# A two-half S5 scan on VectorE: steps in two parts, another order of the work around them, and one weight load issued by ScalarE

## The chip, the cores and the metric

The kernel runs on one core of a Trainium2 chip. A core has five engines that take instructions from queues of their own and wait for each other by semaphores: TensorE (PE) for matrix products, VectorE (DVE), ScalarE (ACT), GpSimd (POOL) and SyncE (SP, which here only issues transfers). The metric is the time of one execution on the device, in microseconds; less is better.

## The reference

A decoder trunk of two layers on 256 tokens of 2048 channels, in float32. Layer 0 is an S5 mixer (a diagonal complex recurrence), layer 1 attention in a sliding window; each is followed by a gated feed-forward network, with root-mean-square norms ahead of every block. The diff touches the S5 mixer alone:

```python
def s5_mixer(u, a_re, a_im, log_step, b_re, b_im, c_re, c_im, d_skip, w_glu):
    ...                                    # lb = exp(a * dt), bb = (lb - 1) / a * b: complex, 128 groups x 64 states
    bu_re = jnp.einsum('blgc,gpc->blgp', uc, bb_re)
    bu_im = jnp.einsum('blgc,gpc->blgp', uc, bb_im)
    ...                                    # s[l] = lb * s[l-1] + bu[l] along the 256 tokens
    y = jnp.einsum('blgp,gcp->blgc', s_re, cr_) - jnp.einsum('blgp,gcp->blgc', s_im, ci_)
    y = y + d_skip.astype(f32) * uf
    g = jax.nn.gelu(y).astype(u.dtype)
    gl = g @ w_glu
    out = gl[..., :dm] * jax.nn.sigmoid(gl[..., dm:])
```

## The kernel before

**Large products.** Every weight is read as pieces of 512 x 512 (`raw`, two buffers, 1 MB each), split into an upper part (`W.high`, ScalarE, line 122) and a lower part (`W.low`, VectorE or GpSimd, line 127), and multiplied with the split activations in three products (lines 922, 923 and 924), 24 matmuls of 128x512 for a piece. `W.load` issues the load of a piece on the sync queue, line 109. From the end of the S5 mixer to the end of the kernel TensorE runs these products.

**S5.** The recurrence is taken in blocks of L = 4 tokens, so there are 64 block states and 62 steps that do work. What enters each block is made on TensorE: `turned_x` transposes the tables X (tile `px`), `tokens` the normed input (tile `pu`), `added` makes the products (tile `pv`), and `kept` copies them into the tiles V0 and V1, one half of the groups each, 4 x 4 copies. The norm's scale r0 comes from sums of squares (`rb`), and `scaled` applies it together with the norm's weights, spread over the partitions by two matmuls into the tile `gb`.

**The scan.** `step(hf)` does one step of half `hf` on VectorE: a multiply of the last state with four tables (line 573; 128 x 128 into the half's PSUM tile `scan`), and two adds into the next state (lines 576 and 578; 128 x 64 each). V0 can start earlier than V1; LEAD = 20 says how far it may be ahead in the code. `copies` moves finished states to the tiles `St` (ScalarE).

**What follows the scan.** For quarters q of the groups: `own_tokens(q)` adds what the block's own tokens give (tile `py`, line 776), `outputs(q)` what the states give (line 798), `activated` is the gelu, `turned` transposes the result (tile `pt`, line 813) and splits it into `gt` (casts on ScalarE, line 820; lower halves on VectorE, line 821). Quarters 0 and 2 belong to V0, 1 and 3 to V1. `early_piece` begins the first linear with the quarters that are there.

**Order.** Tile's dependency tracking sets the semaphores; a scheduler orders what is not pinned. Inside S5 the wrapper `Ordered` (line 210) pins instructions to the order in which the code has them while `on` is true.

Of the kernel before, what the change touches and what calls it, by code (L numbers as in the profile page):

```python
# [9 lines left out]
F32 = mybir.dt.float32  # L10
# [3 lines left out]
ALU = mybir.AluOpType  # L14
# [3 lines left out]
P = 128  # L18
# [11 lines left out]
GC = 16  # L30
# [26 lines left out]
def kernel(  # L57
# [22 lines left out]
    def bank(shape, name="ps"):  # L80
        return ps.tile(shape, F32, tag="ps", name=nm(name))
# [9 lines left out]
    class Weights:  # L91
        def __init__(self):
# [4 lines left out]
            self.limit = 0  # L97

        def add(self, ap):
            self.src.append(ap)  # L100

        def load(self, upto):
            while len(self.raw) < min(upto, len(self.src)):
                i = len(self.raw)
                if i in self.early:
                    t = self.early[i]()
                else:
                    t = pp.tile([P, 4, 512], F32, tag="raw", name=nm("raw"), bufs=2)
                nc.sync.dma_start(t, self.src[i].rearrange("(a p) n -> p a n", p=P))
                self.raw.append(t)  # L110
# [83 lines left out]
    def s5(early_piece):  # L194
# [3 lines left out]
        with st:  # L198
# [24 lines left out]

            Vt = [sp.tile([P, NK, 2, 32], F32, tag=f"V{hf}", name=f"V{hf}") for hf in range(2)]

# [66 lines left out]
            S.copy(Bn[:, 2], Bn[:, 0])  # L292


            gb = [bank([P, 512], "gb") for _ in range(2)]
            for hf in range(2):
                PE.matmul(gb[hf], sel.rearrange("p k h -> p (k h)"), nrow[:, 512 * hf : 512 * hf + 512],
                          start=True, stop=True)

# [81 lines left out]
            V.tensor_scalar(nr, LP[:, 0, 0], -1.0, None, ALU.add)  # L381
            PL.tensor_tensor(u, LP[:, 0, 1], aim, op=ALU.mult)
            PL.tensor_tensor(t, nr, are, op=ALU.mult)
            PL.tensor_tensor(w, nr, aim, op=ALU.mult)
            PL.tensor_tensor(t, t, u, op=ALU.add)
            PL.tensor_tensor(u, LP[:, 0, 1], are, op=ALU.mult)
            PL.tensor_tensor(q_[:, 0], t, iv, op=ALU.mult)
            PL.tensor_tensor(u, u, w, op=ALU.subtract)
            PL.tensor_tensor(q_[:, 1], u, iv, op=ALU.mult)


# [26 lines left out]
            squares(2)  # L418
            turned_b(B2, 1, negated)
            for i in (2, 3):  # L420
                turned_b(B2, i, lambda o, v: V.tensor_scalar(o, v, sgn[:, 1:2], None, ALU.mult))
# [58 lines left out]
            PE.matmul(pss, both.rearrange("p a k -> p (a k)"), ssq, start=True, stop=True)  # L480

            r0, rv2, ry2 = (sp.tile([P, L], F32, name=f"r{i}") for i in range(3))
            token(0, 2)
# [38 lines left out]
            tokens(0, 1)  # L522
            last_token(1)

# [21 lines left out]
            def kept(t, b, copy):  # L546
                p0 = 16 * (b // 2) + 8 * (t % 2) + 4 * (b % 2)
                copy(Vt[t // 2][:, 1:, :, p0 : p0 + 4], pvs[t, b].rearrange("p r a k -> p k r a")[:, : NK - 1])

# [4 lines left out]
            def scan_tables(hf):  # L554
                scan.append(bank([P, 2, 2, 2, 32], "scan"))
                re, im = (LPT[:, 3, ri].rearrange("p (h f a) -> p f h a", h=2, f=2)[:, hf] for ri in range(2))
                for o, v, f in ((0, re, 1.0), (1, re, 1.0), (2, im, 1.0), (3, im, -1.0)):
                    S.mul(scan[hf][:, 0, o // 2, o % 2].rearrange("p (h a) -> p h a", h=2), v, f)

# [36 lines left out]
            turned_x(0, 0)  # L596
            turned_x(0, 1)
            imag_and_tokens(1)
            added(0, 0)
# [38 lines left out]
            PL.tensor_tensor(Cq[:, :, 1], Cq[:, :, 1], c2[:, :, 0], op=ALU.add)  # L638

            lead(4)  # L640
            last_token(2)
# [4 lines left out]
            added(2, 0)  # L646
            kept(2, 0, S.copy)
            turned_x(2, 2)
            added(2, 1)
# [22 lines left out]
            kept(3, 2, S.copy)  # L672

            pc = bank([P, PAIRS], "pc")
            PE.transpose(pc, drows.rearrange("a g j c -> a (g j c)"), ident[:PAIRS, :PAIRS])
            dcol = lp.tile([P, PAIRS], F32, name="dcol")
            S.copy(dcol, pc)
            dd = lp.tile([P, PAIRS, GC], F32, name="dd")
            PL.tensor_tensor(dd, bc(dcol, 2, GC), bc(idm, 1, PAIRS), op=ALU.mult)
# [103 lines left out]
            def copied(q, k0, k1):  # L783
                a = q // 2 * 16
                return S.copy(St[q][:, :, :, k0:k1], Vt[q % 2][:, k0:k1, :, a : a + 16].rearrange("p k r a -> p r a k"))

# [39 lines left out]

            def end(a, b, between=lambda: None):
# [25 lines left out]
            while reached[0] < NK - 1:  # L853
                step(0)
                if reached[0] + 1 in cuts:
# [442 lines left out]
```

## Time and profile before

| | us |
|---|---|
| time, median of 3 runs | 2014.27 (2013.39 to 2014.71) |
| time of the profiled execution | 2014.75 |
| its span, first to last instruction | 2013.0 |
| TensorE busy | 1971.2 (98%) |
| VectorE busy | 1087.0 (54%) |
| ScalarE busy | 857.9 (43%) |
| GpSimd busy | 103.4 (5%) |

The shares are means over the whole span. They mix the first 140 us, in which the S5 mixer is worked out, with 1870 us of products.

### The profile page before, as it was taken

Reading aid. Unit: us, or ns where it says so; the run is one execution under the profiler, and the core shown is the slowest. Engines: PE = TensorE matmul, PEld = TensorE weight load, DVE = VectorE, ACT = ScalarE, POOL = GpSimd, SP = SyncE. Lnnn points to the kernel's source line nnn. Section 1 sums busy time; section 2 is a strip of 40 time slices with the busy share of each in tenths; the row PEclk is TensorE's granted clock in tenths of the full one; section 3 lists DMA queues with packets and bytes.
Section 4 is the critical chain, followed back from the end, with each engine's and each line's share of the span. In section 5 each row is a group of like instructions: output and inputs, shape, how many; then the busy total and the mean of one; then the engine's idle time right before and its main releaser. Section 6 shows DMA issues by size and latency. Waiting matters only on the chain.

```text
span 2013.0 us, 25105 instructions
## 1 busy us (share of the span) xinstructions
PE 1971.2 (98%) x10640; PEld 1633.5 (81%) x10640; DVE 1087.0 (54%) x1343; ACT 857.9 (43%) x871; POOL 103.4 (5%) x77
## 2 busy tenths in 40 slices
PE   7699999999999999999999999999999999999998
PEld 6577888888888888888888888888888888888886
DVE  8964555444444454454566885544454445444445
ACT  6554444333334333433455554433333343343333
POOL 6850000000000000000000000000000000000000
PEclk9899999999999999999999999999999999999999
DMA  4037665565566565555554435566556555655564
GB/s 129 23 109 230 202 202 190 188 188 188 188 189 190 190 198 192 190 188 188 181 196 159 151 126 169 188 189 190 192 192 198 188 188 189 190 190 192 192 198 146
DMA packets 183316, 360.62 MB, mean 179 GB/s; under 512 B 10402, under 2 KB 10466, under 8 KB 183076
## 3 DMA queue, kind: packets, MB, share of 16 engines
q1 hardware_dynamic: 182192, 355.56, 54.8%
q8 instruction: 83, 1.36, 0.3%
q10 hardware_dynamic: 580, 2.14, 0.3%
q0 software_dynamic: 432, 1.33, 0.2%
q14 instruction: 29, 0.24, 0.0%
HBM read 356.90 MB, written 2.10 MB: 178 GB/s over the span
## 4 chain that ended last, share of the span: by engine, by line
PE 93%; DVE 5%; DMA 1%; ACT 1%; issue 0%; POOL 0%; DVEq 0%; ACTq 0%
PE acc L922 29%; PE acc L924 29%; PE acc L923 29%; DVE scan L573 1%; PE tr L1061 1%; DVE V L578 1%; DVE V L576 1%; DMA raw<-in_s_w_glu_dram 1%; DVE w L127 1%; PE pv L210 1%; PE tr L966 1%; PE tr L1196 1%; PE py L798 0%; PE at L1166 0%; PE px L210 0%
## 5 line engine op out<-in xcount | busy, mean ns | idle before, releaser
L127 DVE TENSOR_TENSOR w<-raw,w 128x2048 fp32r<-128x2048 f32 x330 | 757.1, 2294 | 826.3 <-ACT w L122 826.2
L122 ACT ACTIVATE w<-raw 128x2048 fp32r<-128x2048 f32 x332 | 636.2, 1916 | 983.2 <-PE acc L924 834.1
L922 PE MATMUL acc<-w,xT 128*128 128x512 f32 x1568 | 613.1, 391 | 0.0
L924 PE MATMUL acc<-w,xT 128*128 128x512 f32 x1568 | 610.5, 389 | 0.0
L923 PE MATMUL acc<-w,xT 128*128 128x512 f32 x1568 | 610.2, 389 | 0.0
L922 PEld LDWEIGHTS acc<-w,xT 128*128 128x128 f32 x1568 | 294.4, 188 | 62.6 <-issue 2.3
L924 PEld LDWEIGHTS acc<-w,xT 128*128 128x128 f32 x1568 | 294.3, 188 | 61.5
L923 PEld LDWEIGHTS acc<-w,xT 128*128 128x128 f32 x1568 | 294.5, 188 | 60.3
L922 PE MATMUL acc<-w,hT 128*128 128x512 f32 x704 | 275.2, 391 | 0.0
L923 PE MATMUL acc<-w,hT 128*128 128x512 f32 x704 | 273.6, 389 | 0.0
L924 PE MATMUL acc<-w,hT 128*128 128x512 f32 x704 | 273.4, 389 | 0.0
L922 PEld LDWEIGHTS acc<-w,hT 128*128 128x128 f32 x704 | 132.2, 188 | 28.1 <-ACT hT L1063 1.2
L924 PEld LDWEIGHTS acc<-w,hT 128*128 128x128 f32 x704 | 132.1, 188 | 27.6
L923 PEld LDWEIGHTS acc<-w,hT 128*128 128x128 f32 x704 | 132.2, 188 | 27.0
L923 PE MATMUL acc<-w,gt 128*128 128x512 f32 x256 | 99.8, 390 | 0.6 <-DVE w L127 0.6
L922 PE MATMUL acc<-w,gt 128*128 128x512 f32 x256 | 100.1, 392 | 0.0
L924 PE MATMUL acc<-w,gt 128*128 128x512 f32 x256 | 99.7, 389 | 0.0
L923 PEld LDWEIGHTS acc<-w,gt 128*128 128x128 f32 x256 | 48.1, 188 | 10.8 <-DVE w L127 1.0
L1088 DVE TENSOR_TENSOR h<-h,acc 128x512 f32<-128x512 f32 x64 | 43.5, 687 | 24.4 <-PE acc L924 24.4
L924 PEld LDWEIGHTS acc<-w,gt 128*128 128x128 f32 x256 | 48.1, 188 | 10.0
L922 PEld LDWEIGHTS acc<-w,gt 128*128 128x128 f32 x256 | 48.1, 188 | 9.9
L1074 ACT ACTIVATE act<-acc,ry 128x512 f32<-128x512 f32 x44 | 30.1, 690 | 59.9 <-PE acc L924 59.9
(242 smaller groups left out, 1204.6 us busy)
## 6 DMA issues: line engine op xcount, KB each, us to landing
raw<-in_ffn_w_gate_dram SPq DMA_DIRECT2D x88, 1024.0 KB, 5.2
raw<-in_ffn_w_up_dram SPq DMA_DIRECT2D x88, 1024.0 KB, 5.2
raw<-in_ffn_w_down_dram SPq DMA_DIRECT2D x88, 1024.0 KB, 5.1
raw<-in_s_w_glu_dram SPq DMA_DIRECT2D x32, 1024.0 KB, 5.3
raw<-in_attn_w_qkv_dram SPq DMA_DIRECT2D x20, 1024.0 KB, 5.1
raw<-in_attn_w_o_dram SPq DMA_DIRECT2D x16, 1024.0 KB, 5.0
xk<-in_x_dram SPq DMA_DIRECT2D x4, 512.0 KB, 7.1
h<-in_x_dram SPq DMA_DIRECT2D x8, 256.0 KB, 5.8
```

Of the source, the lines that this page charges most:

```text
L122: keep(S.activation(w[:, 0], self.raw[i], AF.Copy))
L127: keep(e.tensor_tensor(lo, self.raw[i], hi.bitcast(F32), op=ALU.subtract))
L210: return (lambda *a, **k: pin(f(*a, **k))) if self.on else f
L573: keep(V.tensor_tensor(t_, ws[..., part], bc(Vt[hf][:, k - 1, :, part], 1, 2), op=ALU.mult))
L576: V.tensor_tensor(v, v, t_[:, 0], op=ALU.add)
L578: V.tensor_tensor(v, v, t_[:, 1, ::-1], op=ALU.add)
L922: keep(PE.matmul(acc, x_[:, 0], w[0][:, a], start=first, stop=False))
L923: PE.matmul(acc, x_[:, 0], w[1][:, a], start=False, stop=False)
L924: PE.matmul(acc, x_[:, 1], w[0][:, a], start=False, stop=last)
L966: PE.transpose(pt[:, t], h[t][:, kt * P : (kt + 1) * P], ident)
L1074: S.activation(s, pg[t], AF.Silu, scale=r[0][:, t : t + 1])
L1088: V.tensor_tensor(hc, hc, acc[t], op=ALU.add)
```

## The change

Four things. First, the tiles V0, V1 and `scan` get an axis of two parts of 16 columns that lie apart, and `step(hf, 2)` does a step in two parts: two multiplies of 128 x 64 and four adds of 128 x 32. V0's steps ahead of V1's first and V1's steps after V0's last are done so; where both run, steps stay whole. Second, things move: the two matmuls on the norm's weights (`gb`) behind the one for the sums of squares, one eviction of B2 from ScalarE to VectorE, the q chain on GpSimd, `last_token(1)`, the small transpose `pc` with `dcol` and `dd`, and the splitting of weight piece 0 into the middle of V1's inputs; the last X tokens are pinned ahead of the first step. Third, the load of weight piece 5 is held back (`hold`) and issued by ScalarE inside `end(1, 3)`. Fourth, with all this the scheduler puts TensorE's work at the end of the scan in another order.

```diff
@@ Weights
+            self.hold = 5
-        def load(self, upto):
-            while len(self.raw) < min(upto, len(self.src)):
+        def load(self, upto, e=nc.sync):
+            while len(self.raw) < min(upto, len(self.src), self.hold):
...
-                nc.sync.dma_start(t, self.src[i].rearrange("(a p) n -> p a n", p=P))
+                ins = e.dma_start(t, self.src[i].rearrange("(a p) n -> p a n", p=P))
+                if e is not nc.sync:
+                    tc.keep_in_program_order(ins)
@@ s5
-            Vt = [sp.tile([P, NK, 2, 32], F32, tag=f"V{hf}", name=f"V{hf}") for hf in range(2)]
+            Vt = [sp.tile([P, NK, 2, 2, 16], F32, tag=f"V{hf}", name=f"V{hf}") for hf in range(2)]
...
-            turned_b(B2, 1, negated)
-            for i in (2, 3):
+            for i in (1, 2, 3):
                 turned_b(B2, i, lambda o, v: V.tensor_scalar(o, v, sgn[:, 1:2], None, ALU.mult))
...
             PE.matmul(pss, both.rearrange("p a k -> p (a k)"), ssq, start=True, stop=True)
+            gb = [bank([P, 512], "gb") for _ in range(2)]
+            for hf in range(2):
+                PE.matmul(gb[hf], sel.rearrange("p k h -> p (k h)"), nrow[:, 512 * hf : 512 * hf + 512],
+                          start=True, stop=True)
...
-                scan.append(bank([P, 2, 2, 2, 32], "scan"))
+                scan.append(bank([P, 2, 2, 2, 2, 16], "scan"))
...
-                n = 32 // parts
-                ws, pr = scan[hf][:, 0], scan[hf][:, 1]
-                vs = []
-                for i in range(parts):
-                    part = slice(n * i, n * (i + 1))
-                    t_ = pr[..., part]
-                    keep(V.tensor_tensor(t_, ws[..., part], bc(Vt[hf][:, k - 1, :, part], 1, 2), op=ALU.mult))
-                    vs.append((Vt[hf][:, k, :, part], t_))
-                for v, t_ in vs:
-                    V.tensor_tensor(v, v, t_[:, 0], op=ALU.add)
-                for v, t_ in vs:
-                    V.tensor_tensor(v, v, t_[:, 1, ::-1], op=ALU.add)
+                each = [slice(i, i + 1) for i in range(2)] if parts == 2 else [slice(0, 2)]
+                for p in each:
+                    ws, pr = (scan[hf][:, i, p].rearrange("p h l r a -> p h l (r a)") for i in range(2))
+                    last = Vt[hf][:, k - 1, p].rearrange("p h r a -> p h (r a)")
+                    keep(V.tensor_tensor(pr, ws, bc(last, 2, 2), op=ALU.mult))
+                for l in range(2):
+                    for p in each:
+                        v, pr = Vt[hf][:, k, p], scan[hf][:, 1, p, l]
+                        V.tensor_tensor(v, v, pr[:, :, ::-1] if l else pr, op=ALU.add)

             def lead(n):
                 for i in range(n):
-                    step(0)
+                    step(0, 2, pin if i == 0 else lambda ins: ins)
...
+            imag_and_tokens(3)
             V.on = False
-            imag_and_tokens(3)
...
+            pc = bank([P, PAIRS], "pc")
+            PE.transpose(pc, drows.rearrange("a g j c -> a (g j c)"), ident[:PAIRS, :PAIRS])
+            dcol = lp.tile([P, PAIRS], F32, name="dcol")
+            S.copy(dcol, pc)
...
             kept(2, 0, S.copy)
+            W.high(0, pin)
+            W.low(0, pin, PL)
...
             kept(3, 3, S.copy)
             lead(2)
-            W.high(0, pin)
-            W.low(0, pin, PL)
...
                 outputs(b, (0,))
                 split_outputs(a, ya)
+                then()
                 outputs(b, (1,), pin)
...
             while reached[0] < NK - 1:
-                step(0)
+                step(0, 1 if reached[1] > 1 else 2)
...
-                    step(1, keep=pin)
+                    step(1, 2, pin)
...
+            def load():
+
+                W.hold = len(W.src)
+                W.load(6, nc.scalar)
+
-            last = end(1, 3, lambda: own_tokens(3))
+            last = end(1, 3, lambda: own_tokens(3), load)
```

The order of the built programs, at three places. In these rows V_77 is V0, V_78 is V1, the tile `scan` with the lower number belongs to V0, "waits DVE_49" is a wait for VectorE's own count, and "x2" two rows that read alike.

VectorE, a step of V1 after V0's last. Before:

```order
L573 TENSOR_TENSOR scan_805<-scan_805,V_78 128x128 [waits DVE_49]
L576 TENSOR_TENSOR V_78<-V_78,scan_805 128x64 [waits DVE_49]
L578 TENSOR_TENSOR V_78<-V_78,scan_805 128x64 [waits DVE_49]
```

With the change:

```order
L564 TENSOR_TENSOR scan_837<-scan_837,V_78 128x64 [waits DVE_49] x2
L568 TENSOR_TENSOR V_78<-V_78,scan_837 128x32 [waits DVE_49]
L568 TENSOR_TENSOR V_78<-V_78,scan_837 128x32
L568 TENSOR_TENSOR V_78<-V_78,scan_837 128x32 [waits DVE_49] x2
```

Six instructions stand for three, and five of them wait for VectorE's count. The second multiply waits for the count that the first one raises, the first add for that of the second multiply.

VectorE, where V1's first multiply comes in (it waits for ScalarE's copy). Before, behind V0's sixteenth step:

```order
L573 TENSOR_TENSOR scan_593<-scan_593,V_77 128x128 [waits DVE_49]
L573 TENSOR_TENSOR scan_805<-scan_805,V_78 128x128 [waits Activation_49]
L576 TENSOR_TENSOR V_77<-V_77,scan_593 128x64 [waits DVE_49]
L576 TENSOR_TENSOR V_78<-V_78,scan_805 128x64 [waits DVE_49]
L578 TENSOR_TENSOR V_77<-V_77,scan_593 128x64 [waits DVE_49]
```

With the change, behind V0's twelfth step:

```order
L564 TENSOR_TENSOR scan_593<-scan_593,V_77 128x64 [waits DVE_49] x2
L564 TENSOR_TENSOR scan_837<-scan_837,V_78 128x128 [waits Activation_49]
L568 TENSOR_TENSOR V_77<-V_77,scan_593 128x32 [waits DVE_49]
L568 TENSOR_TENSOR V_77<-V_77,scan_593 128x32
L568 TENSOR_TENSOR V_77<-V_77,scan_593 128x32 [waits DVE_49] x2
L568 TENSOR_TENSOR V_78<-V_78,scan_837 128x64
```

V1 comes in three steps of V0 earlier in the order, and the first nine steps of V1 stand beside steps of V0 in two parts; then follow 32 pairs of whole steps and nine whole steps of V0 alone.

TensorE, from own_tokens(3) and outputs(1) on (py_2048/2049 and py_2170/2171 are the tiles of quarter 3, T_1223 and T_1268 the tables of quarter 1; lines of what repeats are left out). Before:

```order
L798 MATMUL py_1942<-T_1223,St_1842 64x64 [waits Activation_49,Pool_49]
...
L776 MATMUL py_2048<-M_1443,U 64x64 [waits PE_49]
...
L798 MATMUL py_2048<-T_1232,St_1843 64x64 [waits Activation_49,Pool_49]
...
L813 MATMUL pt_2114<-ident,y_2042 128x128 [waits PE_49,Activation_49]
...
L922 MATMUL acc_1914<-w_1839,gt_1816 128x512
L923 MATMUL acc_1914<-w_1839,gt_1816 128x512 [waits Pool_49]
...
L813 MATMUL pt_2181<-ident,y_2161 128x128 [waits DVE_49,Activation_49]
```

With the change:

```order
L775 MATMUL py_2170<-M_1506,U 64x64 [waits PE_49]
...
L927 MATMUL acc_2038<-w_1929,gt_1906 128x512 [waits Activation_49]
L928 MATMUL acc_2038<-w_1929,gt_1906 128x512 [waits Pool_49]
...
L775 MATMUL py_2171<-M_1506,U 64x64 [waits DVE_49]
L796 MATMUL py_2064<-T_1268,St_1932 64x64 [waits Activation_49]
...
L811 MATMUL pt_2236<-ident,y_2164 128x128 [waits PE_49,Activation_49]
...
L927 MATMUL acc_1883<-w_174_2098,gt_2241 128x512 [waits Activation_49]
...
L811 MATMUL pt_2307<-ident,y_2285 128x128 [waits DVE_49,Activation_49]
```

Sixteen matmuls of own_tokens(3), 12 products of weight piece 3 (w_1839 before, w_1929 now) and three more of own_tokens(3), the first of which waits for VectorE, now stand ahead of outputs(1); the other 12 products of that piece stand behind the last transposes.

## Rows read from the trace of the kernel before

**Rows 1.** Busy time by stage, us from the span's start. Columns: length, then busy us and (in brackets) instructions of PE, PEld (weight loads), DVE, ACT and POOL, the granted clock of TensorE, DMA share, GB/s.

```profile
39.40:56.50 17.10, 15.44 (x321) 13.28 (x321) 12.65 (x50) 12.83 (x29) 5.57 (x3) 1.00 0.21 64
56.50:94.30 37.80, 22.56 (x420) 19.65 (x416) 37.70 (x245) 18.44 (x26) 36.60 (x18) 0.82 0.09 30
200.00:1000.00 800.00, 800.00 (x3585) 663.16 (x3584) 389.84 (x244) 315.09 (x222) 0.00 (x0) 1.00 0.60 192
```

**Rows 2.** The chain that ended last, followed back from 141 us, its shares of that stretch by engine and line.

```profile
by line: DVE scan L573 18.2%; DVE V L578 12.5%; DVE V L576 12.3%; PE pv L210 8.9%; PE py L798 5.7%; issue 5.3%; DVE w L127 5.2%; PE px L210 4.2%; DVE gt L821 2.6%; PE pu L210 2.1%; DMA ls<-in_s_log_step_dram 1.5%; PE pt L813 1.5%; ACT scan 
```

**Rows 3.** VectorE's instructions in order of time, near the end of V1: start, duration, engine, line, operation, written tile <- read tiles, sizes, count.

```profile
122.42 0.30 DVE L573 TENSOR_TENSOR scan<-scan,V 128x128 f32<-128x128 f32 x1
122.75 0.22 DVE L576 TENSOR_TENSOR V<-V,scan 128x64 f32<-128x64 f32 x1
123.01 0.22 DVE L578 TENSOR_TENSOR V<-V,scan 128x64 f32<-128x64 f32 x1
123.26 0.30 DVE L573 TENSOR_TENSOR scan<-scan,V 128x128 f32<-128x128 f32 x1
123.59 0.22 DVE L576 TENSOR_TENSOR V<-V,scan 128x64 f32<-128x64 f32 x1
123.85 0.22 DVE L578 TENSOR_TENSOR V<-V,scan 128x64 f32<-128x64 f32 x1
```

**Rows 4.** The same view where V1 comes in, in the pairs (a row x2 runs from the first's start to the second's end), where V0 is alone again, and where V1 is. In square brackets the idle time of the engine ahead of it, and what ended it.

```profile
56.60 0.30 DVE L573 TENSOR_TENSOR scan<-scan,V 128x128 f32<-128x128 f32 x1 [2.88 <-ACT V L210]
...
60.11 0.49 DVE L573 TENSOR_TENSOR scan<-scan,V 128x128 f32<-128x128 f32 x2
60.51 0.35 DVE L576 TENSOR_TENSOR V<-V,scan 128x64 f32<-128x64 f32 x2
60.77 0.35 DVE L578 TENSOR_TENSOR V<-V,scan 128x64 f32<-128x64 f32 x2
...
94.34 0.29 DVE L573 TENSOR_TENSOR scan<-scan,V 128x128 f32<-128x128 f32 x1
...
98.43 0.29 DVE L573 TENSOR_TENSOR scan<-scan,V 128x128 f32<-128x128 f32 x1
```

**Rows 5.** The same view: four-element instructions of the norm, and the first lower gate halves.

```profile
18.72 0.17 DVE L210 SCALAR_TENSOR_TENSOR rb<-rb,r 128x4 f32<-128x4 f32 x1
18.92 0.16 DVE L210 SCALAR_TENSOR_TENSOR r<-rb,r 128x4 f32<-128x4 f32 x1
19.12 0.48 DVE L210 SCALAR_TENSOR_TENSOR xs<-xk,r,gb 128x256 f32<-128x256 f32 x1
...
104.04 1.29 DVE L821 TENSOR_TENSOR gt<-pt,gt 128x512 fp32r<-128x512 f32 x2 [0.59 <-ACT gt L820]
```

**Rows 6.** TensorE in order of time, from outputs(1) to the first products behind the scan's work. A float32 matmul is two records here.

```profile
124.66 2.09 PE L798 MATMUL py<-T,St 64*64 64x64 f32 x128 [0.48 <-ACT St L785]
126.54 1.14 PE L776 MATMUL py<-M,U 64*64 64x64 f32 x64
...
129.86 1.15 PE L798 MATMUL py<-T,St 64*64 64x64 f32 x61 [2.11 <-issue]
130.94 1.09 PE L813 MATMUL pt<-ident,y 128*128 128x128 f32 x8
131.97 1.14 PE L798 MATMUL py<-T,St 64*64 64x64 f32 x58
133.56 0.34 PE L798 MATMUL py<-T,St 64*64 64x64 f32 x6 [0.45 <-issue]
133.82 0.50 PE L922 MATMUL acc<-w,gt 128*128 128x512 f32 x1
...
136.68 1.04 PE L813 MATMUL pt<-ident,y 128*128 128x128 f32 x8
...
141.48 0.50 PE L923 MATMUL acc<-w,gt 128*128 128x512 f32 x1 [0.57 <-DVE w L127]
```

**Rows 7.** ScalarE in order of time: the last copy into V1 and the upper half of weight piece 0.

```profile
55.19 0.22 ACT L210 COPY dcol<-pc 128x64 f32<-128x64 f32 x1
55.99 0.58 ACT L210 COPY V<-pv 128x504 f32<-128x504 f32 x1 [0.59 <-PE pv L210]
56.47 1.92 ACT L122 ACTIVATE w<-raw 128x2048 fp32r<-128x2048 f32 x1
```

**Rows 8.** TensorE early on, groups of instructions in order of time.

```profile
3.14 3.75 PE L210 MATMUL gb<-nrow,sel 2*128 2x512 f32 x4 [3.14 <-DVE sm L310]
...
16.39 0.39 PE L210 MATMUL rb<-ssq,both 128*128 128x4 f32 x2 [0.44 <-ACT U L210]
20.92 1.94 PE L210 MATMUL pu<-ident,xs 128*128 128x128 f32 x8 [4.15 <-DVE xs L210]
...
24.80 1.67 PE L210 MATMUL pv<-U,xt 64*64 64x64 f32 x32
```

**Rows 9.** Two early stretches by the columns of rows 1.

```profile
12.33:19.16 6.83, 4.00 (x69) 3.65 (x67) 5.41 (x19) 5.32 (x12) 5.46 (x11) 1.00 1.17 281
19.16:26.00 6.84, 5.01 (x38) 4.34 (x40) 6.74 (x14) 2.86 (x5) 6.84 (x8) 0.50 0.05 14
```

**Rows 10.** ScalarE and VectorE at the end of S5: the gelu of quarter 3, its lower gate halves, the lower halves of weight pieces 4 and 5.

```profile
133.99 1.21 ACT L806 ACTIVATE y<-py 128x256 f32<-128x256 f32 x4 [1.29 <-PE py L798]
...
137.94 1.29 DVE L821 TENSOR_TENSOR gt<-pt,gt 128x512 fp32r<-128x512 f32 x2 [4.39 <-ACT gt L820]
139.14 4.48 DVE L127 TENSOR_TENSOR w<-raw,w 128x2048 fp32r<-128x2048 f32 x2
```

**Rows 11.** The sync queue's issues from 120 us on, and the loads of weight pieces in the first 150 us (KB each, median us from issue to landing).

```profile
123.08 20.94 SPq L109 DMA_DIRECT2D raw<-in_s_w_glu_dram  x3
...
raw<-in_s_w_glu_dram SPq DMA_DIRECT2D x8, 1024.0 KB, 5.3
```

More of the change, by code (lines that the diff above doesn't have):

```diff
@@ L292, in s5 @@
             S.copy(Bn[:, 2], Bn[:, 0])
[L295 to L298, printed above, removed]
             V.on = False
@@ L381, in s5 @@
             V.tensor_scalar(nr, LP[:, 0, 0], -1.0, None, ALU.add)
[L382 to L389, printed above, removed]
             ssq = sp.tile([P, L], F32, name="ssq")
@@ L522, in s5 @@
             tokens(0, 1)
-            last_token(1)
             early.close()
@@ L546, in kept @@
             def kept(t, b, copy):
-                p0 = 16 * (b // 2) + 8 * (t % 2) + 4 * (b % 2)
-                copy(Vt[t // 2][:, 1:, :, p0 : p0 + 4], pvs[t, b].rearrange("p r a k -> p k r a")[:, : NK - 1])
+                p0 = 8 * (t % 2) + 4 * (b % 2)
+                copy(Vt[t // 2][:, 1:, b // 2, :, p0 : p0 + 4], pvs[t, b].rearrange("p r a k -> p k r a")[:, : NK - 1])
             scan = []
             def scan_tables(hf):
-                scan.append(bank([P, 2, 2, 2, 32], "scan"))
+                scan.append(bank([P, 2, 2, 2, 2, 16], "scan"))
                 re, im = (LPT[:, 3, ri].rearrange("p (h f a) -> p f h a", h=2, f=2)[:, hf] for ri in range(2))
                 for o, v, f in ((0, re, 1.0), (1, re, 1.0), (2, im, 1.0), (3, im, -1.0)):
-                    S.mul(scan[hf][:, 0, o // 2, o % 2].rearrange("p (h a) -> p h a", h=2), v, f)
+                    S.mul(scan[hf][:, 0, :, o // 2, o % 2], v, f)
             reached = [1, 1]
@@ L566, in step @@
                 k = reached[hf]
-                n = 32 // parts
-                ws, pr = scan[hf][:, 0], scan[hf][:, 1]
-                vs = []
-                for i in range(parts):
-                    part = slice(n * i, n * (i + 1))
-                    t_ = pr[..., part]
-                    keep(V.tensor_tensor(t_, ws[..., part], bc(Vt[hf][:, k - 1, :, part], 1, 2), op=ALU.mult))
-                    vs.append((Vt[hf][:, k, :, part], t_))
-                for v, t_ in vs:
-                    V.tensor_tensor(v, v, t_[:, 0], op=ALU.add)
-                for v, t_ in vs:
-                    V.tensor_tensor(v, v, t_[:, 1, ::-1], op=ALU.add)
+                each = [slice(i, i + 1) for i in range(2)] if parts == 2 else [slice(0, 2)]
[7 more added lines that the diff above has]
+                        V.tensor_tensor(v, v, pr[:, :, ::-1] if l else pr, op=ALU.add)
             def lead(n):
                 for i in range(n):
-                    step(0)
+                    step(0, 2, pin if i == 0 else lambda ins: ins)
+            PL.tensor_tensor(u, LP[:, 0, 1], aim, op=ALU.mult)
+            PL.tensor_tensor(t, nr, are, op=ALU.mult)
+            PL.tensor_tensor(w, nr, aim, op=ALU.mult)
+            PL.tensor_tensor(t, t, u, op=ALU.add)
+            PL.tensor_tensor(u, LP[:, 0, 1], are, op=ALU.mult)
+            PL.tensor_tensor(q_[:, 0], t, iv, op=ALU.mult)
+            PL.tensor_tensor(u, u, w, op=ALU.subtract)
+            PL.tensor_tensor(q_[:, 1], u, iv, op=ALU.mult)
             for t in (2, 3):
@@ L597, in s5 @@
             turned_x(0, 1)
+            last_token(1)
             imag_and_tokens(1)
@@ L638, in s5 @@
             PL.tensor_tensor(Cq[:, :, 1], Cq[:, :, 1], c2[:, :, 0], op=ALU.add)
+            pc = bank([P, PAIRS], "pc")
+            PE.transpose(pc, drows.rearrange("a g j c -> a (g j c)"), ident[:PAIRS, :PAIRS])
+            dcol = lp.tile([P, PAIRS], F32, name="dcol")
+            S.copy(dcol, pc)
+            dd = lp.tile([P, PAIRS, GC], F32, name="dd")
+            PL.tensor_tensor(dd, bc(dcol, 2, GC), bc(idm, 1, PAIRS), op=ALU.mult)
             lead(4)
@@ L672, in s5 @@
             kept(3, 2, S.copy)
[L674 to L679, printed above, removed]
             added(3, 3)
@@ L783, in copied @@
             def copied(q, k0, k1):
-                a = q // 2 * 16
-                return S.copy(St[q][:, :, :, k0:k1], Vt[q % 2][:, k0:k1, :, a : a + 16].rearrange("p k r a -> p r a k"))
+                return S.copy(St[q][:, :, :, k0:k1], Vt[q % 2][:, k0:k1, q // 2].rearrange("p k r a -> p r a k"))
             gt = {}
@@ L825, in split_outputs, with end @@
                     turned(2 * q + mm, ys[mm], pin)
-            def end(a, b, between=lambda: None):
+            def end(a, b, between=lambda: None, then=lambda: None):
                 outputs(a)
```

## Prediction, made before the changed kernel had run

> **What bounds the kernel now.** I read the busy time by stage first [rows 1]. From 200 us on TensorE is busy all of the time (800.00 of 800.00 us, at full clock), and the products there are not touched by the diff. Whatever happens before moves that block as a whole, so the time changes by what the first product of the dense stretch moves: the matmul at 141.48 that follows the wait for the lower half of weight 4 [rows 6]. Ahead of it stands S5. From 56.50 to 94.30 VectorE is busy 37.70 of 37.80 us [rows 1], and the chain back from 141 us goes through the scan's three lines with 18.2 + 12.5 + 12.3% [rows 2]: the recurrence on VectorE is the bound, with TensorE's finishing work behind it.
>
> The scan has two halves, V0 and V1, of 62 steps each. A step alone is a multiply and two adds, each waiting for the one before: starts at 122.42, 122.75, 123.01, next step 123.26, so 0.33 + 0.26 + 0.25 = 0.84 us [rows 3]. With both halves under way, the other's instruction fills the gap: two multiplies take 0.49 us from the first's start, one alone 0.29, so the second starts 0.20 behind; two adds 0.35 against 0.22, so 0.13 behind; 41 such pairs run from 56.60 to 94.34, 0.92 us a pair [rows 3, 4]. V0 runs 16 steps alone before V1 is there, V1's first multiply waits 2.88 us for its input at 56.60, and V0 needs 5 more steps after the pairs (94.34 to 98.43) [rows 4]. V1 then has 21 alone, with lower halves of gates and weights between them, and ends at 123.85 + 0.22 = 124.07 [rows 3].
>
> **The change, term by term.** The sum is made for the start of the dense stretch.
>
> *A step in two parts.* It issues six instructions for three. If the parts ran freely, their latencies would overlap. But the order printed by the build says that the second multiply waits for VectorE's own count, and the count it waits for is the one that the first multiply raises; the first add waits for the second multiply; only the second add goes without. The two parts have the same tile of the scan between them. So both multiplies are paid in series. Prices: four-element instructions that depend on each other start 0.20 us apart [rows 5], 64-element adds 0.255; on that line a 32-element add is 0.226 and a 64-element multiply 0.33 - 0.06 = 0.27. The two first adds start about 0.10 apart (0.20 for 128 elements, 0.13 for 64 [rows 4]). A split step is 0.27 + 0.27 + 0.10 + 0.226 + 0.226 = 1.09 us against 0.84: +0.24. If the waits cost nothing, it is bounded below by 0.27 + 0.226 + 0.226 = 0.72 (-0.12).
>
> The Trainium skill, VectorE: DVE Perf Modes, section "The DRAIN you can't avoid", says that a VectorE instruction does not start until the pipe of the one before is empty, and that leaving out a semaphore gains nothing (it grants an earlier start to one that is not held). By that a split step would be 2 x 0.27 + 4 x 0.226 = 1.44 us. The pairs disagree: six instructions in 0.92 us where the same six in a row take 1.68 [rows 3, 4]. I go by the rows.
>
> *V1 ready.* Its last input copy ends at 56.57 [rows 7]. The ScalarE copy of weight 0's upper half (1.92 us [rows 7]) moves from behind it to between V1's copies, while the 0.22 us copy of dcol leaves that queue; I take +1.45 for both, since ScalarE is busy 12.83 of 17.10 us there and cannot hide it all [rows 1] (bounds 0 and 1.92). Against it, the two matmuls on the norm's weights go from the start (3.75 us for both [rows 8]) into TensorE's idle stretch before the first token transposes, 4.15 us long [rows 8]: from 16.8 the first is done at 18.7, ahead of the scaling at 19.12 that reads it [rows 5], and the second at 20.5 at the latest, ahead of the transposes at 20.92. The clock is granted in full (2.4 GHz) until 19.16 and at half (1.2 GHz) until 26.00 [rows 9], with the engine idle just ahead of the fall. Eight transposes took 1.94 us and the first 32 products 1.67 there [rows 8]; with the clock kept, the chain to the scan's first input is shorter by about 1.05 us (bounds 0 and 1.05). Net +0.4.
>
> *V0's end.* The order has 12 split steps of V0 alone (free, since VectorE waits there), the 13th step's two multiplies, then V1. Nine steps pair a split V0 with a whole V1: following the waits, 0.27 + 0.33 + 0.10 + 0.22 + 0.22 = 1.14 against 0.92, so 9 x 0.22 = +2.0. V0 now starts 12 steps ahead and not 16, so four more whole steps stand alone at the end: 4 x 0.84 = +3.4; the two multiplies ahead give 0.5 back. Together +4.9.
>
> *V1 alone.* 21 split steps x 0.24 = +5.1. The wait of 0.59 us for the first gate halves [rows 5] is covered by the longer six steps: -0.6. V1 ends at 124.07 + 0.4 + 4.9 + 5.1 - 0.6 = 133.9.
>
> *From V1's end to the dense stretch.* Before: 141.48 - 124.07 = 17.4 us. After V1's end there stood the second half of the last states' copies, 2.09 of outputs(1), 1.14 of own tokens, outputs(3) in two pieces round the transposes, 12 products of weight 3 between 133.82 and 136.68, 8 transposes, 12 more products, and a wait for weight 4's lower half; and 2.11 us that are put down to nothing but issue [rows 6]. The changed order puts 12 of those products and 19 of the 32 own-token instructions ahead of V1's end, and the last transposes right behind the gelu. I count from V1's end: 0.59 (copy), 2.09, 0.47, 1.12, 1.09, 1.15 puts outputs(3) done at +6.5; gelu 1.21, the cast, the gate's lower halves and weight 4's first lower half follow as before (133.99 gelu, 137.94 gate, 139.14 weight [rows 6, 10], less the 2.1 us in which transposes and cast stood behind 12 products): products resume at +12.0. I leave 0.5 for issue gaps (bounds 0 and the 2.6 seen: 2.11 and 0.45). 12.5 against 17.4: -4.9. Hidden cover: the 12 products ahead are done while TensorE waits for V1; without that wait they would cost their 2.7 us again.
>
> *Weight 5.* Its load goes from the sync queue (issued at 123.08 [rows 11]) to ScalarE behind the gate casts, at about 140. At a median 5.3 us to land [rows 11] and 1.92 + 2.2 to split, its lower half is there near 150, before weight 4's 24 products, twice the 2.7 us that 12 take [rows 6], end at 151.8. What is queued behind the issue on ScalarE is the last gelu; the issue counts next to nothing. Price 0; were the cover gone, each us late would be one.
>
> Sum: 133.9 + 12.5 = 146.4 against 141.48, **+4.9 us**. The profiled execution took 2014.75 us (span 2013.0); 2019.65 by it, and 2019.2 by the median of 2014.27, which is 0.48 lower. About 0.2%, 4.0 us, is what a measurement of this kernel can tell from no change.
>
> **Rivals.**
> - *The split's waits are free* (not slower). A V1 step is 0.72: 21 x -0.12 = -2.5, V1 ends at 126.9. Then TensorE decides: its dense work before outputs(1), moved by V0's +5.3 to about 129 with own tokens, plus 2.7 and 0.6 brought ahead, ends at 132.5; +12 gives 144.4, so +2.9: 2017.2, inside 0.2%. It decides if the second multiply starts less than 0.15 behind the first. Paired rows show that spacing, but for instructions that wait for others.
> - *TensorE stays slow or stalls* (slower still): half clock remains to 26 (+1.05), the 2.1 us issue gap stays as it lies near weight 5's transfer and may belong to code that is fetched (+2.1): 2022.3.
> - *Instructions never overlap*, not even in the split parts: a split step is then 1.44, so 9 x 0.52 + 3.4 - 0.5 = +7.6 for V0's end and 21 x 0.60 = +12.6 for V1; with +0.4, -0.6 and -4.9 that is +15: 2029. The pairs speak against it. It is what the section named above would make of the change.
> - *Faster*: it needs 4 us that I find no single row for; free waits, no issue gaps at the end (-0.5) and V1 ready 1 us sooner together reach +1. Kept for what I misread.
>
> **How the numbers follow.** My sum 0.50, with its own range 2017.2 to 2021.2 (V1 ready 55.9 to 58.5, issue gaps 0 to 2.6; a fifth of it under 2018.3), free waits 0.18, slow TensorE 0.14, never overlapping 0.03, faster 0.15. Slower: 0.40 + 0.14 + 0.03 = 0.57; same: 0.10 + 0.18 = 0.28; faster 0.15. The range reaches from 2014.5 (below free waits by the clock's gain and the bounds of issue) to 2023.5.
>
> **What would show it.** A split step alone at 1.09 us, its second multiply 0.27 behind its first; V1's first multiply at 57.0; V0's last add near 103.6; V1's end at 134; TensorE idle about 1.5 us before outputs(1), none of 2 us behind it; the granted clock full between 19 and 26; products resuming near 146. The prediction is wrong if split steps take 0.75, or if the wait for V1 is hidden on TensorE.

## The result, and the profile with the change

The changed kernel takes 2020.5 us (median of 7 runs, 2019.31 to 2021.66) against 2013.69 (7 runs taken with it): a ratio of 1.0031, 95% interval 1.0019 to 1.0043. It is slower, by about 6 us (6.2 by the ratio, 6.8 by the two medians). The profiled execution took 2020.7 us with a span of 2018.9, 5.9 longer than before. The forecast was 2019.2, with a range from 2014.5 to 2023.5.

VectorE with the change, in order of time: start, duration, engine, line, operation, tiles, sizes, count (a row x2 or x4 runs from the first's start to the last's end); in brackets the idle time ahead and what ended it. Split steps of V0 alone, V1's first multiply, mixed steps, V0's last whole steps, and V1 alone to its end. They answer to [rows 3, 4]:

```profile
51.55 0.50 DVE L564 TENSOR_TENSOR scan<-scan,V 128x64 f32<-128x64 f32 x2
52.09 0.51 DVE L568 TENSOR_TENSOR V<-V,scan 128x32 f32<-128x32 f32 x4
52.63 0.50 DVE L564 TENSOR_TENSOR scan<-scan,V 128x64 f32<-128x64 f32 x2
57.69 0.30 DVE L564 TENSOR_TENSOR scan<-scan,V 128x128 f32<-128x128 f32 x1 [4.56 <-ACT V L214]
...
58.44 0.23 DVE L564 TENSOR_TENSOR scan<-scan,V 128x64 f32<-128x64 f32 x1
...
59.59 0.23 DVE L564 TENSOR_TENSOR scan<-scan,V 128x64 f32<-128x64 f32 x1
...
104.09 0.30 DVE L564 TENSOR_TENSOR scan<-scan,V 128x128 f32<-128x128 f32 x1
104.42 0.48 DVE L568 TENSOR_TENSOR V<-V,scan 128x64 f32<-128x64 f32 x2
104.81 0.49 DVE L564 TENSOR_TENSOR scan<-scan,V 128x64 f32<-128x64 f32 x2
...
133.41 0.51 DVE L568 TENSOR_TENSOR V<-V,scan 128x32 f32<-128x32 f32 x4
```

A split step is 52.63 - 51.55 = 1.08 us against 0.84 for a whole one. Its two multiplies take 0.50 from the first's start and one takes 0.23, so the second starts 0.27 behind. A mixed step is 59.59 - 58.44 = 1.15. V1's first multiply comes at 57.69 (+1.09), V1 is alone from 104.81 (+6.38), and its last add ends at 133.41 + 0.51 = 133.92 (+9.85).

TensorE with the change, by the same columns, from the end of the early products to the dense stretch, as in [rows 6]:

```profile
130.18 2.09 PE L775 MATMUL py<-M,U 64*64 64x64 f32 x96
132.20 0.50 PE L927 MATMUL acc<-w,gt 128*128 128x512 f32 x1
...
134.83 0.39 PE L929 MATMUL acc<-w,gt 128*128 128x512 f32 x1
...
135.43 2.03 PE L796 MATMUL py<-T,St 64*64 64x64 f32 x123
137.24 0.74 PE L775 MATMUL py<-M,U 64*64 64x64 f32 x19
139.23 0.27 PE L775 MATMUL py<-M,U 64*64 64x64 f32 x2 [1.25 <-issue]
...
140.54 1.10 PE L811 MATMUL pt<-ident,y 128*128 128x128 f32 x8
...
142.95 0.46 PE L796 MATMUL py<-T,St 64*64 64x64 f32 x16 [0.45 <-issue]
...
144.17 1.21 PE L811 MATMUL pt<-ident,y 128*128 128x128 f32 x8
145.13 0.48 PE L927 MATMUL acc<-w,gt 128*128 128x512 f32 x1
...
149.02 0.50 PE L928 MATMUL acc<-w,gt 128*128 128x512 f32 x1 [0.89 <-DVE w L131]
```

The dense stretch starts at 149.02, 7.54 us later than before. When V1 ends, at 133.92, TensorE is still at the products that were brought ahead: the first starts at 132.20, the twelfth at 134.83, and the first matmul behind them at 135.15, with no gap before or behind them.

Of the 7.54 us, 1.6 are given back later, in one place. TensorE's waits from the dense stretch to 200 us (engine, line, what it waited for: us in total, times, longest), first before and then with the change:

```profile
PE tr L966 <- DVE h L1049: 2.0, 2, 1.7
```

```profile
PE tr L971 <- DVE h L1054: 0.3, 1, 0.3
```

Before, the first transposes of the next block's input (`h`) wait 2.0 us for VectorE, which has the lower half of a weight to make first (166.07 to 168.36); with the change 0.3. From the first dense product to the end it is 2013.0 - 141.48 = 1871.5 before and 2018.9 - 149.02 = 1869.9 with the change. Without that wait both are 1869.5 to 1869.6.

### The profile page after: what moved, and what is told of

It reads as the page before. It is cut to its first block, busy times and chain, and to the rows that moved or that the text cites. A ratio compares the mean times of both kernels' runs of the same rounds, so it can differ in the third digit from the quotient of the medians.

```text
span 2018.9 us, 25227 instructions
## 1 busy us (share of the span) xinstructions
PE 1972.3 (98%) x10640; PEld 1634.8 (81%) x10640; DVE 1096.5 (54%) x1470; ACT 857.6 (42%) x870; POOL 100.4 (5%) x77
## 4 chain that ended last, share of the span: by engine, by line
PE 94%; DVE 4%; DMA 1%; ACT 1%; issue 0%; SPq 0%; DVEq 0%; ACTq 0%
PE acc L927 30%; PE acc L929 29%; PE acc L928 29%; DVE V L568 2%; DVE scan L564 1%; DMA raw<-in_s_w_glu_dram 1%; PE tr L1066 1%; PE pv L214 1%; PE tr L971 1%; PE tr L1201 1%; PE at L1171 0%; ACT w L126 0%; PE py L796 0%; DVE w L131 0%; PE ps L214 0%
```

## The experiments

Each run is compared with the kernel before on the same chip, and its ratio given with a 95% interval. Two runs can come from two chips, and the intervals are about 2 us to either side, so a difference of 1 or 2 us between two runs is no more than likely.

**Whole steps, and split steps alone.** Two runs part the split from everything else. The first takes the changed kernel and makes all steps whole:

```diff
-                each = [slice(i, i + 1) for i in range(2)] if parts == 2 else [slice(0, 2)]
+                each = [slice(0, 2)]
```

> The changed kernel with every scan step whole again (three instructions), all else as changed. Theory (the two serial multiplies of a split step, and the order that the scheduler makes of them, cost the time): V0's last step and V1's first alone come back to about 99 us, V1's end to about 125, and the time to within 1.5 us of the kernel before (2013 to 2015.5). Rival (the moved work costs it: weight 0's upper half between V1's copies, the norm's weights, the load by ScalarE): it stays 4 us or more above the kernel before.

2013.57 us, ratio 0.9996 (0.9987 to 1.0006): the loss is gone. V1 starts at 56.35, V0 ends at 97.3 and V1 at 124.0, and the dense stretch starts at 140.59.

The second takes the kernel before and gives it the two-part tiles and the split steps, nothing else:

```diff
-                step(0)
+                step(0, 1 if reached[1] > 1 else 2)
...
-                    step(1, keep=pin)
+                    step(1, 2, pin)
```

> The kernel before with nothing but the two-part tiles and the split steps. Theory: V1's first multiply stays at 56.6, V0's end is about 5 us later than before, V1's end about 9, and the time is 4 to 6 us above the kernel before. Rival (the moved work costs it): at most 1.5 us above.

2019.76 us, ratio 1.0025 (1.0015 to 1.0034): the loss is there without the moved work. V1's first multiply stays at 56.64, V0 ends 5.7 us later than before (104.13) and V1 9 us later, and the dense stretch starts at 147.82. The rival in which the moved work costs the time falls.

**Which of the split steps.** V1's steps whole, V0's lead split:

```diff
-                    step(1, 2, pin)
+                    step(1, 1, pin)
```

> The changed kernel with V1's 21 steps alone whole, V0's lead still split. The sum's term (21 x 0.24 = 5.1 us, less the 0.6) makes it 4.5 us faster than the changed kernel. Rival, from the changed kernel's trace (TensorE was busy without a gap until outputs(1), so V1's end was not what it waited for): only 1 to 2.5 us faster, the six steps ahead of the first gate halves and what the order at the end makes of it.

2018.57 us, ratio 1.0021 (1.0012 to 1.0030): 1.9 us less than the changed kernel, as the rival had it, and not 4.5. The two intervals overlap, so the 1.9 is a best figure only; 4.5 less would be a ratio of 1.0009, below this run's interval. The other way round, V0 whole and V1 alone split:

```diff
-                    step(0, 2, pin if i == 0 else lambda ins: ins)
+                    step(0, 1, pin if i == 0 else lambda ins: ins)
...
-                step(0, 1 if reached[1] > 1 else 2)
+                step(0, 1)
```

> The changed kernel with V0's steps whole and V1's 21 steps alone in two parts. The sum gives V0's end back (4.9 us): 1 to 2 us above the kernel before. By the reading of the changed kernel's trace (V0's end moves all of TensorE's work, V1's end is hidden for the most part) the same or a little less: 0.5 to 2 us above.

2014.11 us, ratio 0.9999 (0.9990 to 1.0008): no loss, though V1's 21 split steps end about 2.7 us later than the whole ones before, at 126.8. Split steps in V1 cost next to nothing, split steps in V0 nearly everything. TensorE in this run:

```profile
121.93 2.09 PE L775 MATMUL py<-M,U 64*64 64x64 f32 x96
...
126.90 0.44 PE L775 MATMUL py<-M,U 64*64 64x64 f32 x6
127.21 2.10 PE L796 MATMUL py<-T,St 64*64 64x64 f32 x128
...
140.12 0.50 PE L928 MATMUL acc<-w,gt 128*128 128x512 f32 x1 [0.89 <-DVE w L131]
```

The 12 products stand between the own tokens and 126.90, so TensorE had work until V1's states were there, and the dense stretch starts at 140.12, earlier than before the change.

**The moved work.** Three runs take back one move each in the changed kernel: weight 5 loaded from the sync queue, weight 0's halves made behind V1's inputs again, and the matmuls on the norm's weights at the start again.

```diff
-            self.hold = 5
+            self.hold = 10**9
...
-                W.hold = len(W.src)
-                W.load(6, nc.scalar)
+                pass
```

> The changed kernel with weight 5 loaded from the sync queue as before. The sum prices the load by ScalarE at nothing: the same as the changed kernel within 1 us. Rival (the gap of about 2 us on TensorE in outputs belongs to that transfer, and the changed kernel avoids it): 0.5 to 2 us slower than the changed kernel.

2020.35 us, ratio 1.0026 (1.0015 to 1.0038): no difference from the changed kernel. Without the load by ScalarE the gaps by issue on TensorE are 0.9 and 1.4 us in all, no longer than with it (1.2 and 1.6), so they don't belong to that transfer. The traces hold a better candidate. One DMA queue (q8, of kind instruction) moves instructions, 16 KB at a time. All 44 gaps by issue that TensorE has between 95 and 200 us in the twelve traces of this case end 1.2 to 1.6 us behind the landing of such a transfer: before the change the one of 2.11 us ends at 129.86, 1.40 behind a transfer from 127.42 to 128.46, and with it the one of 1.25 us ends at 139.23, 1.49 behind one from 136.33 to 137.74. So TensorE most likely waits there for its own code; no run tested it.

```diff
             kept(2, 0, S.copy)
-            W.high(0, pin)
-            W.low(0, pin, PL)
...
             lead(2)
+            W.high(0, pin)
+            W.low(0, pin, PL)
```

> The changed kernel with weight 0's upper and lower half made behind V1's last input copy again. By the prediction's term (1.45 us for V1's readiness, all on VectorE's path) V1's first multiply comes at about 56 and the time 1 to 1.5 us below the changed kernel. Rival (GpSimd's long chain of state tables then starts 3 to 4 us later again, and the copies of V1's states wait for it): no gain, GpSimd's last table near 115 and not 111.

2019.47 us, ratio 1.0026 (1.0015 to 1.0037). V1's first multiply comes at 55.73, as expected, and GpSimd's tables end at 115.4, as the rival said; the time is 1 us less, within the intervals. Inconclusive in the time. How much of V1's start is the weight's is read below, from runs whose clock fell at the same place.

```diff
             S.copy(Bn[:, 2], Bn[:, 0])
+            gb = [bank([P, 512], "gb") for _ in range(2)]
...
             PE.matmul(pss, both.rearrange("p a k -> p (a k)"), ssq, start=True, stop=True)
-            gb = [bank([P, 512], "gb") for _ in range(2)]
```

> The changed kernel with the two matmuls on the norm's weights at the start again. By the prediction's term (the clock stays full through the first tokens, 1.05 us) this is about 1 us slower than the changed kernel. Rival, from the traces taken so far (half clock for about 6 us between 18 and 27 in all of them, with the matmuls moved or not, only the start of it differs): no difference beyond 0.5 us.

2019.98 us, ratio 1.0028 (1.0018 to 1.0039): no difference from the changed kernel. The clock in the changed kernel, by the columns of [rows 1]:

```profile
12.33:19.16 6.83, 6.49 (x73) 4.90 (x71) 5.79 (x18) 4.92 (x11) 3.62 (x4) 1.00 1.17 276
19.16:26.00 6.84, 4.96 (x38) 4.28 (x40) 6.71 (x14) 2.80 (x5) 6.68 (x13) 0.59 0.06 19
26.00:39.40 13.40, 13.07 (x273) 11.40 (x269) 12.66 (x22) 9.17 (x21) 13.38 (x8) 0.96 0.01 3
```

TensorE is busier between 12.33 and 19.16 (6.49 us; 4.00 before [rows 9]), but the two matmuls take 1.98 us in their new place (16.88 to 18.86), not the 3.75 of the start, and the engine still stands idle 2.1 us ahead of the first token transposes. The granted clock falls to half all the same, from 20.35 to 27.15; before the change from 19.15 to 26.00.

That it comes later here is not the work of the move. In each of the twelve traces the clock stands at half once in this stretch, for 6.8 us; it falls somewhere between 17.4 and 20.35, and kernels with the move lie at both ends. The changed kernel and the run with weight 5 on the sync queue have the same code until long after this stretch, and theirs fall at 20.35 and 18.95. In the run with whole steps (matmuls moved, first pair of rows) and in this run (matmuls back, second pair) it falls at the same 17.4 and comes back at 24.2, and V1's first multiply stands at 56.35 and 56.31:

```profile
18.00:20.00 2.00, 0.67 (x1) 0.00 (x0) 1.76 (x8) 0.00 (x0) 2.00 (x3) 0.50 0.74 279
24.00:26.00 2.00, 2.00 (x40) 1.69 (x38) 2.00 (x5) 1.86 (x4) 2.00 (x3) 0.95 0.03 8
```

```profile
18.00:20.00 2.00, 0.00 (x0) 0.00 (x0) 1.83 (x8) 0.00 (x0) 2.00 (x3) 0.50 0.75 289
24.00:26.00 2.00, 2.00 (x40) 1.68 (x38) 2.00 (x5) 1.86 (x4) 2.00 (x3) 0.95 0.03 8
```

```profile
56.35 0.30 DVE L564 TENSOR_TENSOR scan<-scan,V 128x128 f32<-128x128 f32 x1 [3.06 <-ACT V L214]
```

```profile
56.31 0.30 DVE L565 TENSOR_TENSOR scan<-scan,V 128x128 f32<-128x128 f32 x1 [4.50 <-ACT V L214]
```

**Multiplies without a tile in common.** The products go to tiles of their own, one for each part, in SBUF; nothing in the code then makes the second multiply of a step wait for the first:

```diff
+            prods = [[sp.tile([P, n, 2, 2, 16], F32, name=f"prod{hf}{i}") for i, n in enumerate((1, 1, 2))]
+                     for hf in range(2)]
...
-                    ws, pr = (scan[hf][:, i, p].rearrange("p h l r a -> p h l (r a)") for i in range(2))
+                    ws = scan[hf][:, 0, p].rearrange("p h l r a -> p h l (r a)")
+                    tl = prods[hf][p.start if len(each) == 2 else 2]
+                    got.append(tl)
+                    pr = tl.rearrange("p h l r a -> p h l (r a)")
```

> The changed kernel with the products of the scan's multiplies in tiles of their own (one for each part, in SBUF) and not in the PSUM tile of the tables, so that the second multiply has no tile in common with the first one's result. Theory (the serial multiplies are the price of the split): a split step takes 0.72 to 0.78 us, V0 has its whole lead of 20 before V1 starts, V0 ends near 97 and V1 near 120, and the time is 1 to 4 us below the kernel before. Rival (VectorE runs one instruction after the other whatever the waits say): a split step stays over 1.0 us and the time near the changed kernel's.

2064.75 us, ratio 1.0250 (1.0235 to 1.0266), which neither theory had said. VectorE and GpSimd in this run, by the same columns:

```profile
39.76 5.98 DVE L574 TENSOR_TENSOR V<-V,prod 128x32 f32<-128x32 f32 x4
45.67 0.34 DVE L570 TENSOR_TENSOR prod<-scan,V 128x64 f32<-128x64 f32 x2
45.93 4.64 DVE L574 TENSOR_TENSOR V<-V,prod 128x32 f32<-128x32 f32 x4
50.51 0.35 DVE L570 TENSOR_TENSOR prod<-scan,V 128x64 f32<-128x64 f32 x2
50.78 0.53 DVE L574 TENSOR_TENSOR V<-V,prod 128x32 f32<-128x32 f32 x4
51.23 0.34 DVE L570 TENSOR_TENSOR prod<-scan,V 128x64 f32<-128x64 f32 x2
51.50 0.53 DVE L574 TENSOR_TENSOR V<-V,prod 128x32 f32<-128x32 f32 x4
51.95 0.35 DVE L570 TENSOR_TENSOR prod<-scan,V 128x64 f32<-128x64 f32 x2
```

```profile
43.77 1.92 POOL L214 TENSOR_TENSOR dd<-dcol,idm 128x1024 f32<-128x1024 f32 x1
45.66 4.54 POOL L214 TENSOR_TENSOR w<-raw,w 128x2048 fp32r<-128x2048 f32 x1
59.40 2.07 POOL L722 TENSOR_TENSOR tmpT<-Cg,LPT 128x1024 f32<-128x1024 f32 x1 [9.21 <-DVE prod L570]
```

Two things are read from it. While GpSimd is idle (50.2 to 59.4) a split step takes 51.95 - 51.23 = 0.72 us, and the second multiply starts 0.12 behind the first: the serial multiplies are the price of the split, and without their wait it is what the lower bound had said. The products lie in another memory here too, but that by itself doesn't make a multiply shorter: one alone takes 0.22 us into SBUF (at 39.62) and 0.23 into PSUM (at 58.44 in the changed kernel). And while GpSimd works, the adds, both of whose inputs now lie in SBUF, stand still: four of them take 5.98 us, to the moment when GpSimd changes from one instruction to the next (45.66), and 4.64 during the next one. The adds that are held up end at 41.49, 43.86, 45.75 and 50.25, each 0.05 us behind the end of a GpSimd instruction. Products in PSUM are what keeps VectorE clear of GpSimd. The Trainium skill, SBUF — State Buffer, section "SBUF: two separate sides", says that a VectorE instruction with two inputs in SBUF and a GpSimd instruction that reads SBUF exclude each other for a whole instruction; this trace agrees, with 5.98 and 4.64 us. A split with products in four PSUM banks was not tried.

**Steps of V0 ahead of V1.** In the changed kernel VectorE stands idle 4.56 us ahead of V1's first multiply, and 2.88 before [rows 4]. In the code V1's first step stands behind V0's 21st, but the scheduler had put it behind the 16th (with the change behind the 12th split one). Here all steps are whole (by the edit of the first run), LEAD is 19, and V0's steps and V1's first are pinned, which makes 20 steps ahead:

```diff
-LEAD = 20
+LEAD = 19
...
-                step(0, 1 if reached[1] > 1 else 2)
+                step(0, 1, pin if reached[1] == 1 else lambda ins: ins)
...
-                    step(1)
+                    step(1, 1, pin if reached[1] == 1 else lambda ins: ins)
```

> The changed kernel with whole steps everywhere, and V0's steps and V1's first step pinned so that V0 has done 20 steps (not 16) when V1 starts; before, VectorE stood idle for 3 us there. Theory (what counts is how many steps VectorE still has to do when V1 is ready, since TensorE's work hangs on V0's end): 42 pairs follow and nothing of V0 alone; V0's end comes 3.2 us earlier than with 16, about 95, V1's end 4 us earlier, about 120, and the time is 2 to 3.5 us below that of the whole steps without the pin, 2010 to 2012. Rival (the end of S5 is held by something else, the weights or the code): under 1 us.

2011.44 us, ratio 0.9981 (0.9972 to 0.9990): faster than the kernel before by 2.8 us (by the medians; 3.8 by the ratio), and than whole steps without the pin by 2.1. VectorE, ScalarE and TensorE:

```profile
57.34 0.50 DVE L564 TENSOR_TENSOR scan<-scan,V 128x128 f32<-128x128 f32 x2 [0.84 <-ACT V L214]
```

```profile
112.91 7.68 ACT L783 COPY St<-V 128x896 f32<-128x896 f32 x6
```

```profile
137.34 0.50 PE L928 MATMUL acc<-w,gt 128*128 128x512 f32 x1 [0.57 <-DVE w L131]
```

VectorE waits only 0.84 us for V1 (which comes at 57.34, 1 us later than in the run with whole steps, as the half clock does: from 19.85 and not from 17.4), and the dense stretch starts at 137.34, 4.1 us earlier than before. Of that, 1.9 are lost again: 2010.7 - 137.34 = 1873.4, against 1871.5 before. The wait in the same place as before (transposes for h) is 0.3 longer, 2.3 us. The rest fits TensorE's clock: the longest piece of that wait, 2.12 us, ends at 166.50, and from 166.6 to 170.0 the granted clock stands at half, which it does not behind the wait of 1.70 before the change. Seven transposes take 1.75 us there and 0.98 before. Whether all eleven executions of this kernel (2009.18 to 2012.54) have this half clock no trace says; the profiled one, 2012.48, is among the slowest.

The same pin in the kernel before, with none of the moved work:

> The kernel before with nothing but the same pin: 20 steps of V0 ahead of V1's first. Theory: the same 2 to 3.5 us below the kernel before. Rival (the gain needs the moved work too, since the three steps meet the other instructions of VectorE and ScalarE): under 1 us.

2013.98 us, ratio 0.9997 (0.9988 to 1.0006): nothing gained, as the rival had it. V1 ends at 120.1, 4 us earlier, but ScalarE and TensorE in this run say what is next:

```profile
115.39 8.23 ACT L785 COPY St<-V 128x896 f32<-128x896 f32 x8 [3.67 <-POOL tmpT L717]
```

```profile
123.45 3.57 PE L798 MATMUL py<-T,St 64*64 64x64 f32 x128 [2.03 <-ACT St L785]
```

The copies of V1's states wait for GpSimd, until 115.4, and then take 8.2 us; TensorE waits 2.03 for them. With weight 0 and dd moved ahead, GpSimd's tables start at 59.4 and not at 62.4, and in the run before this one the copies start at 112.91. So the moved work alone gains nothing measurable, the pin alone gains nothing, and both together gain 2.8 us. I read it as two chains of nearly the same length that end there, VectorE's and the one through GpSimd's tables.

## Why the prediction was right, and where its working was not

**The split step** (forecast 1.09, measured 1.08; second multiply 0.27 behind, measured 0.27; mixed step 1.14, measured 1.15) was right, and with it the cause: the run with whole steps takes the loss away, split steps alone bring it. That the multiplies are paid in series because they wait for each other is shown by the run without the wait (0.72; the lower bound said 0.72). The rival in which instructions never overlap has 1.44 for both; neither trace shows that. (It prices a mixed step too low as well: nine instructions one after the other are 1.44 + 0.84 = 2.28.)

**V1 ready** was forecast at +0.4 and came at +1.09. The part that failed is the clock: 1.05 us were to be gained and none were. The two matmuls were to fill TensorE's idle stretch to 20.5; they filled it to 18.86, and the granted clock still went to half for 6.8 us. Putting them back changes nothing. The 1.45 for weight 0 was too much: with the half clock from 17.9 in both, V1 starts at 56.50 with the weight moved (the run with V0 whole) and at 55.73 without, so 0.8.

```profile
56.50 0.30 DVE L564 TENSOR_TENSOR scan<-scan,V 128x128 f32<-128x128 f32 x1 [3.06 <-ACT V L214]
```

```profile
55.73 0.43 DVE L564 TENSOR_TENSOR scan<-scan,V 128x128 f32<-128x128 f32 x2 [4.30 <-ACT V L214]
```

About half of the 1.09 belongs to the profiled execution and not to the change. In the seven traces that have weight 0 moved and the products in PSUM, V1 starts the later the later the clock falls: 56.31 and 56.35 (fall at 17.4), 56.50 (17.9), 56.84 (18.65), 56.98 (18.95), 57.34 (19.85), 57.69 (20.35). The first token transposes start near 20.8 in all of them, so a half clock that begins later covers more of the work. With the fall at 19.15, where it was before, they give about 57.1 (an estimate between two of these), +0.5: near the forecast, by two errors that cancel.

**V0's end** was forecast at 4.9 us more from V1's start and came at 104.81 - 57.69 less 98.43 - 56.60, that is +5.3. V1 comes in four steps of V0 earlier in the order, 12 and not 16, as this term had it; the section on the change says three.

**V1 alone** was forecast at +4.5 and came at 29.1 - 25.6 = +3.5. 21 x 0.23 = 4.8 less the 0.59 is 4.2; the rest fits the second of VectorE's lower halves of a weight, which took 3.02 us before, with a GpSimd instruction under way when it started, and 2.29 now, when GpSimd is idle. The forecast of V1's end, 133.9, was met (133.92) by errors that cancel.

**From V1's end to the dense stretch** is the term that was mis-sized: 12.5 forecast, 15.1 measured. TensorE was to stand idle about 1.5 us ahead of outputs(1), and it had no gap at all: its own work, which starts with V0's end, runs until 135.15, after V1's end and the copy that follows it. That is 0.6; issue gaps of 1.7 us, for which 0.5 was left, are 1.2 more; the own tokens and outputs up to the last gelu (143.46) take 0.7 longer than counted; from there on the 5.6 us are as forecast. So the sum's picture, in which V1's end releases everything, was wrong in this place, and the prediction had named that as a sign of being wrong: the wait for V1 is hidden on TensorE. V1's 5.1 us stood in the sum as lost time, though TensorE covers most of them: about 1.9 us is what whole steps there are worth, and V1 split with V0 whole costs nothing measurable. What sets the time is V0's end, which moved by 6.4, against a time of 6 us.

**After the dense stretch starts** the sum had nothing, and 1.6 us came back: the wait for h was 2.0 before and is 0.3 now. In the other runs it lies between 0.3 and 2.3. That it absorbs part of any shift is what the traces show; what decides its length was not tested.

**The number.** The cause was forecast and is shown; that the time came within 1.3 us of 2019.2 is in part luck. The dense stretch was to start 4.9 us later and started 7.5 later, and the 1.6 that came back behind it made good for most of the miss. The sum's own range doesn't come out of its bounds either: taken at both ends they give 2017.6 to 2022.8, not 2017.2 to 2021.2.

**The rivals.** Free waits is not this kernel: its step of 0.72 us was seen only where the wait had been taken away. Slow TensorE was about right in both of its conditions, since the clock fell to half and 1.7 us of issue gaps remained; the measured 2020.5 lies between the sum's 2019.2 and its 2022.3. Faster did not happen; but a reading that I passed by, VectorE's idle 2.88 us ahead of V1, was worth 2.8 us of time with the moved work in place.

## What to carry to other kernels

Before splitting a chain's step to overlap its latencies, look at which counts the instructions wait for: two parts that share a PSUM tile were still put in series here, and then more instructions only cost more. Where two chains on one engine alternate, fill the wait ahead of the second with steps of the first and hold that order; the scheduler may not. And a profile is one execution: where the clock falls differs from one to the next, so compare a start of 1 us more or less between traces whose clock falls at the same place. Last, a change that frees one of two chains of equal length shows nothing until the other is freed too, so try them together.

## What had not been expected of the hardware

VectorE adds of 128x32 with both inputs in SBUF took 5.98 us for four while GpSimd was at work, and 0.53 when it was idle. The granted clock of TensorE stood at half for 6.8 us between 17 and 28 us in every trace of this case, with the two matmuls moved into the idle time ahead of it or not; it fell between 17.4 and 20.35, and V1's start moved with it, by up to 1.4 us. And every gap by issue on TensorE between 95 and 200 us ended 1.2 to 1.6 us behind the landing of a transfer of instructions.
